# Indexer products and sums per pair of heads in a two-layer decoder trunk

## Chip, cores and metric

One core of one Trainium2 chip. The metric is device time in microseconds (us), the median of three executions of one launch.

## The reference

A decoder trunk of two layers on x of 512 tokens by 1024 channels, all in float32: a gated linear recurrence (HGRN2) and a convolutional FFN, then sparse attention (DSA) and a second FFN, and a final norm. The change lies in the sparse attention, whose indexer picks for each query the 128 keys (512 // 4) that it may attend to:

```python
proj = x @ w_in                       # q 1024 | k 128 | v 128 | q_idx 512 | k_idx 64 | w_idx 8
dots = jnp.einsum('bthd,bsd->bths', qib, k_idx)                      # 8 index heads of 64
scores = jnp.einsum('bths,bth->bts', jax.nn.relu(dots), wb)          # sum over the heads
scores = jnp.where(admissible[None], scores, NEG_BIG)                # causal
_, sel = lax.top_k(scores, top_k)
```

The 16 attention heads then take a softmax over the selected keys, with a bias by relative position.

## The kernel before, in words

Every float32 matrix product is made of three `fp32r` matmuls (high times high, high times low, low times high), so a projection block of 128 output channels is 24 matmuls of 128x512 on TensorE (`proj_T`, lines 169 to 171, tile `pj`). Its weight block comes by DMA (`wunit`, line 150) and is split into `whi` and `wlo`. From the projection of k on, ScalarE makes `whi` (L159) and a negative copy (L158), and a DMA on GpSimd's queue adds the weights once more onto that (L160).

TensorE runs its instructions in the order in which the program writes them (`manual_schedule`). That order comes from generators: `weave` runs a main generator, and after each step lets the generators in `side` advance by as much assumed time as the step had; a generator that needs something waits until a name stands in `done`. The order on the other engines is set by the scheduler of the language, which also places all waits.

The sparse layer goes like this:

- `head_in` projects k_idx and w_idx (72 channels), then the four pairs of index heads (b = 0 to 3, 128 channels each). After each pair, `stack` (L675 to L678) writes the pair's two heads as stacked high and low halves into `qh` and `ql`: two copies on ScalarE (L675, L676), then two subtractions on VectorE (L677 ends `qh`, L678 ends `ql`). `kw_evac` (L696, L704 to L706) does the same for the keys, and `kw_weights` turns the weights of the heads (L713, L715).
- `dots`, added to `side` when `head_in` is over, goes through the query blocks t = 1, 2, 3 of 128 queries each; block 0 needs no selection. For a block it goes through the four pairs: four matmuls into two PSUM banks `pi` (L749), a relu on ScalarE (L759), and a multiply-add into the block's sum `sc[t]` on VectorE (L755 for the first head, L760 for the others). Then GpSimd masks the block (L762).
- `top` finds the 128 largest by 16 rounds of MAX (8 largest, L774) and MATCH_REPLACE (L776) on VectorE, first for block 1, then for blocks 2 and 3; at the end a mask `sel1`, `sel2`, `sel3` is written (L779).
- `rest_in` projects k, v and the eight query blocks q0 to q7; each block's PSUM is read by a scaling row on VectorE (`scaled`, L696).
- `attend`, woven into the rest of these projections, takes attention in units of two query blocks and two heads: `scores` (L860 adds the mask by a matmul, L863 multiplies), a biased minimum on VectorE (L870), exponents on ScalarE, and later transposes (L912, L915), copies (L916) and the product with v (L923, L926).

The lines around which the change turns are these:

```python
def head_in():
    pk = yield from proj_T(w_in, O_KI, 72)
    for b in range(4):
        o = yield from proj_T(w_in, O_QI + b * P, hook=({7: lambda: kw_evac(pk)}, {2: kw_weights}, None, None)[b])
        lo_engine[0] = nc.gpsimd
        stack(4 + b, o, nc.vector)
```

Of the kernel before, what the change touches and what calls it, by code (L numbers as in the profile page):

```python
# [8 lines left out]
F32 = mybir.dt.float32  # L9
# [3 lines left out]
AF = mybir.ActivationFunctionType  # L13
ALU = mybir.AluOpType
# [3 lines left out]
P = 128  # L18
D = 1024
T = 512  # L20
# [3 lines left out]
NEG = -1e30  # L24
# [24 lines left out]
def trunk(ctx: ExitStack, tc: tile.TileContext, xT, vecs, convs, hgrn_w_in, hgrn_w_out, dsa_w_in, dsa_w_out,  # L49
          rel_bias, ffn_w_up, ffn_w_down, c_masks, c_onehot, out, dbg=None, stop=99):  # L50
    nc = tc.nc
# [9 lines left out]
    def bank(name):  # L61
        return ps.tile([P, 512], F32, name=name, tag="bank")
# [110 lines left out]
    def proj_T(w, c0, n=P, hook=None):  # L173

        wh, wl = wunit(w[:, c0:c0 + n], KB, n)
        o = bank("pj")
        for k in range(KB):
            mm3(o[:n], wh[:, k, :], wl[:, k, :], xh[:, k, :], xl[:, k, :], k == 0, k == KB - 1)
            yield 0.65
            if hook and k in hook:  # L180
                hook[k]()
        return o


    side, done = [], set()

    def add_side(gen, rate=1.0):
        side.append([gen, rate, 0.0])
# [8 lines left out]
    def weave(gen):  # L197
        for c in gen:
            for e in list(side):
                e[2] += c * e[1]  # L200
                while e in side and e[2] > 0:
                    step(e)
# [458 lines left out]
    with ExitStack() as sx:  # L661
        ds_ = sx.enter_context(tc.tile_pool(name="ds", bufs=1))
        bias = ds_.tile([P, AH, T], F32, name="bias")
        qh = ds_.tile([P, KB, T], F32R, name="qh")
        ql = ds_.tile([P, KB, T], F32R, name="ql")
# [5 lines left out]
        def stack(b, src, lo):  # L671

            a, c = qh[:, b, :], ql[:, b, :]
            top_, bot = rows2
            nc.scalar.activation(a[top_], src[top_], AF.Copy)  # L675
            nc.scalar.activation(c[bot], src[bot], AF.Copy)  # L676
            lo.tensor_tensor(a[bot], src[top_], a[top_].bitcast(F32), op=ALU.subtract)  # L677
            lo.tensor_tensor(c[top_], src[bot], c[bot].bitcast(F32), op=ALU.subtract)  # L678
# [4 lines left out]
        wN = ds_.tile([P, TT, 8], F32, name="wN")  # L683
        scs = ds_.tile([P, 9 * P], F32, name="scs")
        sc = [None, scs[:, 7 * P:], scs[:, 4 * P:7 * P], scs[:, :4 * P]]
        m8 = ds_.tile([P, TT, 8], F32, name="m8")

        with ExitStack() as sy:
            iy = sx.enter_context(tc.tile_pool(name="iy", bufs=1))
            ix = sy.enter_context(tc.tile_pool(name="ix", bufs=1))  # L690
            ki_h = ix.tile([P, T], F32R, name="ki_h")
            ki_l = ix.tile([P, T], F32R, name="ki_l")
# [8 lines left out]
            def kw_evac(o):  # L701
                tmp = scaled(o, 72)
                for r in (slice(0, 64), slice(64, 128)):
                    nc.scalar.activation(ki_h[r], tmp[:64], AF.Copy)  # L704
                nc.vector.tensor_tensor(ki_l[:64], tmp[:64], ki_h[:64].bitcast(F32), op=ALU.subtract)
                nc.vector.tensor_tensor(ki_l[64:], tmp[:64], ki_h[:64].bitcast(F32), op=ALU.subtract)  # L706
                kw.append(tmp)

            def kw_weights():
                tmp = kw.pop()  # L710
                pw = bank("pw")
                for t in range(TT):
                    nc.tensor.transpose(pw[:, t * 72:(t + 1) * 72], tmp[:72, t * P:(t + 1) * P], ident[:72, :72])  # L713
                for t in range(TT):
                    nc.vector.tensor_scalar(wN[:, t, :], pw[:, t * 72 + 64:(t + 1) * 72], 8 ** -0.5 * 64 ** -0.5,  # L715
                                            rstd_c[:, t:t + 1], op0=ALU.mult, op1=ALU.mult)

            def setup():

                yield 7.0  # L720
                nc.vector.tensor_copy(identb, ident)
                nc.gpsimd.memset(vf, 0.0)
                for h in range(0, AH, 4):
                    nc.scalar.activation(bias[:, h:h + 4, :256], far[:, h:h + 4, None].to_broadcast([P, 4, 256]),
                                         AF.Copy, scale=-1.0)

                    back = ix.tile([P, 4, 256], F32, name="back", bufs=2)
                    nc.sync.dma_start(back, bass.AP(tensor=Z.tensor, offset=Z.offset + h * BAND,
                                                    ap=[[1, P], [BAND, 4], [1, 256]]))
                    nc.scalar.activation(bias[:, h:h + 4, 256:], back[:, :, ::-1], AF.Copy)  # L730
                    yield 3.0
# [4 lines that stand above are left out]
                    o = yield from proj_T(w_in, O_QI + b * P,  # L736
                                          hook=({7: lambda: kw_evac(pk)}, {2: kw_weights}, None, None)[b])
                    lo_engine[0] = nc.gpsimd
                    stack(4 + b, o, nc.vector)

            def dots():
                for t in range(1, TT):
                    w = (t + 1) * P
                    ts_ = slice(t * P, (t + 1) * P)
                    for b in range(4):
                        o = [bank("pi") for _ in range(2)]
                        for k_ in (ki_h, ki_l):
                            for e in range(2):
                                nc.tensor.matmul(o[e][:, :w], (qh, ql)[e][:, 4 + b, ts_], k_[:, :w],  # L749
                                                 start=k_ is ki_h, stop=k_ is ki_l)  # L750
                        yield 0.22 * (t + 1)
                        for e in range(2):
                            i = 2 * b + e
                            if i == 0:
                                nc.vector.tensor_scalar(sc[t], o[e][:, :w], 0.0, wN[:, t, 0:1],  # L755
                                                        op0=ALU.max, op1=ALU.mult)
                            else:
                                r_ = ix.tile([P, T], F32, name="relu", bufs=2)
                                nc.scalar.activation(r_[:, :w], o[e][:, :w], AF.Relu)  # L759
                                nc.vector.scalar_tensor_tensor(sc[t], r_[:, :w], wN[:, t, i:i + 1], sc[t],  # L760
                                                               op0=ALU.mult, op1=ALU.add)
                    nc.gpsimd.affine_select(sc[t][:, w - P:], sc[t][:, w - P:], pattern=[[-1, P]], base=0,  # L762
                                            channel_multiplier=1, compare_op=ALU.is_ge, fill=NEG)
                    done.add(f"sc{t}")
                    if t == 1:
                        add_side(top((1,)), 0.4)

            def top(ts):

                while any(f"sc{t}" not in done for t in ts):  # L770
                    yield 0.5
                for r in range(16):
                    for t in ts:
                        nc.vector.max(m8[:, t, :], sc[t])  # L774
                    for t in ts:
                        nc.vector.match_replace(sc[t], m8[:, t, :], sc[t], -3e38)  # L776
                    yield sum(2 * (0.065 + (t + 1) * P / 960) for t in ts)
                for t in ts:
                    nc.vector.tensor_scalar(sel[t], sc[t], -2e38, -NEG, op0=ALU.is_gt, op1=ALU.mult)  # L779
                    done.add(f"sel{t}")  # L780
                if 3 not in ts:
                    add_side(top((2, 3)), 0.55)
# [16 lines left out]
            def rest_in():  # L799
                lo_engine[0] = None  # L800
                pk = yield from proj_T(w_in, O_K)
                pv = yield from proj_T(w_in, O_V, hook={3: lambda: k_out(pk)})
                for b in range(KB):
                    lo_engine[0] = nc.vector if b >= 6 else None
                    o = yield from proj_T(w_in, b * P, hook={3: lambda: kw.append(scaled(pv)), 7: v_out}
                                          if b == 0 else None)
                    tmp = scaled(o, P, -0.125)
                    stack(b, tmp, nc.gpsimd)
                    done.add(f"q{b}")
                done.add("q8")  # L810

            add_side(norm_chain())
            add_side(setup())
            weave(head_in())
            add_side(dots(), 1.0)
            rest = rest_in()
            for c in rest:
                weave([c])
# [220 lines left out]
```

## Time and profile before

| | |
|---|---|
| Median of three executions | 1273.68 us (1273.42 to 1275.24) |
| The profiled execution | 1276.48 us, of which the span from first to last instruction is 1274.7 us |
| Mean granted TensorE clock | 0.997 of full speed |
| Busy, share of the span | TensorE 98%, VectorE 63%, ScalarE 47%, GpSimd 11% |
| Sparse layer | its projections begin at 668 us, its last products with v start at 852 us |

In a timeline row the first number is the start in us from the span's start, the second the length, then engine, line, operation, written and read tiles, sizes; a bracket at the end is idle time of that engine just before, and what ended it. A matmul's end is modelled, so a row of 0.39 us may be followed by the next start 0.23 us after its own. Waits are inferred from semaphore events.

### The profile page before, as it was taken

How to read it: one execution, taken by the hardware profiler on the slowest of the kernel's cores; microseconds unless marked ns; L12 is line 12 of the kernel's file. 1: busy time of each engine (PE TensorE's matmuls, PEld its weight loads, DVE VectorE, ACT ScalarE, POOL GpSimd, SP SyncE). 2: the span in 40 equal slices, each digit the busy share in tenths (PEclk: the TensorE clock that was granted, in tenths of full speed). 3: DMA queues.
4: the chain of work that ended last, by engine and by line, in shares of the span. 5: the costliest groups of instructions: out<-in, count | busy, mean ns of one | idle time of the engine just before them, and what ended most of it. 6: DMA issues, size and time to landing. Idle time of an engine off the chain costs nothing.

```text
span 1274.7 us, 15695 instructions
## 1 busy us (share of the span) xinstructions
PE 1251.4 (98%) x6054; PEld 1046.2 (82%) x6054; DVE 803.0 (63%) x1305; ACT 599.6 (47%) x989; POOL 138.8 (11%) x120
## 2 busy tenths in 40 slices
PE   8999999999999999999999998999999999999997
PEld 7788888887888888888887777988888888888887
DVE  7755777756777777742444999635677777762331
ACT  5546565444544444421337757853444444441430
POOL 3022223110000000000003453300000000000000
PEclk9999999999999999999999999999999999999999
DMA  6339777323333333322237850003233333333222
GB/s 199 117 73 158 133 129 126 76 66 99 91 93 98 99 99 99 98 91 93 87 103 173 134 109 25 27 1 99 83 100 99 99 99 94 92 95 99 91 75 66
DMA packets 199178, 124.05 MB, mean 97 GB/s; under 512 B 5264, under 2 KB 188480, under 8 KB 199104
## 3 DMA queue, kind: packets, MB, share of 16 engines
q1 hardware_dynamic: 170320, 108.31, 28.7%
q0 software_dynamic: 28080, 14.16, 9.3%
q8 instruction: 47, 0.77, 0.3%
q10 hardware_dynamic: 704, 0.58, 0.2%
q14 instruction: 27, 0.22, 0.1%
HBM read 120.92 MB, written 2.12 MB: 97 GB/s over the span
## 4 chain that ended last, share of the span: by engine, by line
PE 88%; DVE 7%; ACT 2%; issue 1%; DMA 0%; POOL 0%; DVEq 0%; SPq 0%; POOLq 0%; ACTq 0%
PE pj L169 17%; PE pj L171 17%; PE pj L170 17%; PE px L169 9%; PE px L171 9%; PE px L170 9%; PE pav L923 2%; DVE scs L776 2%; PE pl L556 1%; PE po L602 1%; DVE m L774 1%; DVE scs L760 1%; PE pl L863 1%; PE pt L912 1%; PE pn L170 1%
## 5 line engine op out<-in xcount | busy, mean ns | idle before, releaser
L169 PE MATMUL pj<-x,whi 128*128 128x512 f32 (+1 forms) x1016 | 403.0, 397 | 0.0
L171 PE MATMUL pj<-x,wlo 128*128 128x512 f32 (+1 forms) x1016 | 396.9, 391 | 1.1 <-DMA wlo<-in_dsa_w_in_dram 1.1
L170 PE MATMUL pj<-x,whi 128*128 128x512 f32 (+1 forms) x1016 | 396.3, 390 | 0.0
L144 DVE TENSOR_TENSOR wlo<-wr,whi 128x1024 fp32r<-128x1024 f32 (+2 forms) x165 | 202.0, 1224 | 155.1 <-ACT whi L143 153.1
L143 ACT ACTIVATE whi<-wr 128x1024 fp32r<-128x1024 f32 (+1 forms) x167 | 173.6, 1039 | 257.1 <-PE px L170 155.2
L171 PEld LDWEIGHTS pj<-x,wlo 128*128 128x128 f32 (+1 forms) x1016 | 190.6, 188 | 42.4 <-DMA wlo<-in_dsa_w_in_dram 1.5
L169 PEld LDWEIGHTS pj<-x,whi 128*128 128x128 f32 (+1 forms) x1016 | 191.0, 188 | 39.2 <-issue 1.6
L170 PEld LDWEIGHTS pj<-x,whi 128*128 128x128 f32 (+1 forms) x1016 | 191.1, 188 | 38.8 <-issue 1.0
L169 PE MATMUL px<-ah,whi 128*128 128x512 f32 (+1 forms) x332 | 128.5, 387 | 0.0
L171 PE MATMUL px<-ah,wlo 128*128 128x512 f32 (+1 forms) x332 | 127.5, 384 | 0.0
L170 PE MATMUL px<-al,whi 128*128 128x512 f32 (+1 forms) x332 | 126.2, 380 | 0.0
L348 DVE TENSOR_TENSOR ub<-pj,rstd_r 128x512 f32<-128x512 f32 x88 | 60.6, 688 | 82.3 <-PE pj L171 77.3
L143 ACT ACTIVATE ah<-c 128x512 fp32r<-128x512 f32 x44 | 27.8, 631 | 115.9 <-DVE c L360 115.9
L171 PEld LDWEIGHTS px<-ah,wlo 128*128 128x128 f32 x332 | 62.3, 188 | 13.5
L170 PEld LDWEIGHTS px<-al,whi 128*128 128x128 f32 x332 | 62.3, 188 | 12.8
L351 ACT ACTIVATE c<-ub,convc 128x512 f32<-128x512 f32 x88 | 71.2, 809 | 2.4 <-DVE ub L348 1.6
L169 PEld LDWEIGHTS px<-ah,whi 128*128 128x128 f32 x332 | 62.4, 188 | 11.4
L353 DVE SCALAR_TENSOR_TENSOR c<-ub,convc,c 128x512 f32<-128x512 f32 x88 | 66.2, 752 | 3.0
L358 ACT ACTIVATE c<-c 128x512 f32<-128x512 f32 x44 | 27.8, 632 | 80.8 <-DVE c L353 80.7
L352 DVE SCALAR_TENSOR_TENSOR c<-ub,convc,c 128x512 f32<-128x512 f32 x88 | 65.6, 746 | 0.0
L522 DVE TENSOR_TENSOR qk<-qk,ftree 128x512 f32<-128x512 f32 x56 | 39.6, 709 | 17.6 <-PE pl L560 7.1
L144 DVE TENSOR_TENSOR al<-c,ah 128x512 fp32r<-128x512 f32 x44 | 30.4, 692 | 29.3 <-ACT ah L143 29.3
(226 smaller groups left out, 1743.9 us busy)
## 6 DMA issues: line engine op xcount, KB each, us to landing
wr<-in_ffn_w_up_dram SPq DMA_DIRECT2D x88, 512.0 KB, 3.8
wr<-in_ffn_w_down_dram SPq DMA_DIRECT2D x41, 512.0 KB, 3.7
wr<-in_hgrn_w_in_dram SPq DMA_DIRECT2D x30, 512.0 KB, 4.1
wlo<-in_hgrn_w_in_dram POOLq DMA_DIRECT2D x19, 512.0 KB, 7.5
wr<-in_dsa_w_in_dram SPq DMA_DIRECT2D x14, 512.0 KB, 3.7
wr<-in_hgrn_w_out_dram SPq DMA_DIRECT2D x8, 512.0 KB, 3.6
wlo<-in_dsa_w_in_dram POOLq DMA_DIRECT2D x8, 512.0 KB, 7.8
wr<-in_dsa_w_out_dram SPq DMA_DIRECT2D x8, 512.0 KB, 3.8
```

The lines of the kernel that those rows point to most:

```text
L143: nc.scalar.activation(dst_h, src, AF.Copy)
L144: lo.tensor_tensor(dst_l, src, dst_h.bitcast(F32), op=ALU.subtract)
L169: nc.tensor.matmul(o, ah, bh, start=start, stop=False)
L170: nc.tensor.matmul(o, ah, bl, start=False, stop=False)
L171: nc.tensor.matmul(o, al, bh, start=False, stop=stop)
L348: nc.vector.tensor_tensor(u[:, 2:], o, rows(), op=ALU.mult)
L351: nc.scalar.activation(c, u[:, 2:], AF.Identity, scale=cc[2], bias=cc[3])
L352: nc.vector.scalar_tensor_tensor(c, u[:, 1:T + 1], cc[1], c, op0=ALU.mult, op1=ALU.add)
L353: nc.vector.scalar_tensor_tensor(c, u[:, 0:T], cc[0], c, op0=ALU.mult, op1=ALU.add)
L358: nc.scalar.activation(g, g, AF.Silu)
L522: nc.vector.tensor_tensor(turned(m), turned(m), factors(ft, m), op=ALU.mult)
L776: nc.vector.match_replace(sc[t], m8[:, t, :], sc[t], -3e38)
```

## The change

`dots` becomes a generator of one pair: it goes through the three query blocks for that pair, and is added to `side` as soon as the pair is projected and its `stack` is written, in place of once after `head_in`. It waits until the heads' weights are there (`done.add("wN")`). The mask of a block, and the start of `top`, follow the last pair. The matmuls, relus, sums and masks are the same in number and size.

```diff
@@ kw_weights
                                             rstd_c[:, t:t + 1], op0=ALU.mult, op1=ALU.mult)
+                done.add("wN")
@@ head_in
                     stack(4 + b, o, nc.vector)
-
-            def dots():
+                    add_side(dots(b))
+
+            def dots(b):
+
+                while "wN" not in done:
+                    yield 0.3
                 for t in range(1, TT):
                     w = (t + 1) * P
                     ts_ = slice(t * P, (t + 1) * P)
-                    for b in range(4):
-                        o = [bank("pi") for _ in range(2)]
-                        for k_ in (ki_h, ki_l):
-                            for e in range(2):
-                                nc.tensor.matmul(o[e][:, :w], (qh, ql)[e][:, 4 + b, ts_], k_[:, :w],
-                                                 start=k_ is ki_h, stop=k_ is ki_l)
-                        yield 0.22 * (t + 1)
...
+                    o = [bank("pi") for _ in range(2)]
+                    for k_ in (ki_h, ki_l):
                         for e in range(2):
+                            nc.tensor.matmul(o[e][:, :w], (qh, ql)[e][:, 4 + b, ts_], k_[:, :w],
+                                             start=k_ is ki_h, stop=k_ is ki_l)
+                    yield 0.22 * (t + 1)
...
+                    if b == 3:
+                        nc.gpsimd.affine_select(sc[t][:, w - P:], sc[t][:, w - P:], pattern=[[-1, P]], base=0,
+                                                channel_multiplier=1, compare_op=ALU.is_ge, fill=NEG)
+                        done.add(f"sc{t}")
+                        if t == 1:
+                            add_side(top((1,)), 0.4)
@@
             weave(head_in())
-            add_side(dots(), 1.0)
             rest = rest_in()
```

Lines of the changed kernel: the product is L753 there, the first head's sum L759, the relu L763, the other sums L764, MAX L779, MATCH_REPLACE L781, the masks L784, the biased minimum L874.

**First place: TensorE in the projection of pair 1**, after the transposes of the heads' weights (`pw`, L713), which follow that projection's ninth matmul. Before:

```order
L171 MATMUL pj<-x,wlo 128x512
L713 MATMUL pw<-ident,tmp 128x72 x4
L169 MATMUL pj<-x,whi 128x512
L170 MATMUL pj<-x,whi 128x512
L171 MATMUL pj<-x,wlo 128x512
L169 MATMUL pj<-x,whi 128x512
```

And now:

```order
L171 MATMUL pj<-x,wlo 128x512
L713 MATMUL pw<-ident,tmp 128x72 x4
L169 MATMUL pj<-x,whi 128x512
L170 MATMUL pj<-x,whi 128x512
L171 MATMUL pj<-x,wlo 128x512
L753 MATMUL pi<-ki_h,qh 128x256
L753 MATMUL pi<-ki_h,ql 128x256
L753 MATMUL pi<-ki_l,qh 128x256
L753 MATMUL pi<-ki_l,ql 128x256
```

The first products of pair 0 stand three projection matmuls after `pw`. For pairs 1, 2 and 3 the first products stand three matmuls after the end of that pair's own projection. Before, the first of all products stood three matmuls after the end of pair 3's.

**Second place: VectorE before the mask `sel1`** (`sel_5019`). Before, from the scaling row of q2 on:

```order
L696 SCALAR_TENSOR_TENSOR tmp<-pj,rstd_r 128x512
L774 MAX m_5025<-scs 128x8
L776 MATCH_REPLACE scs<-m_5025,scs 128x512
L776 MATCH_REPLACE scs<-m_5025,scs 128x256
L774 MAX m_5025<-scs 128x8
L779 TENSOR_SCALAR sel_5019<-scs 128x256
```

And now:

```order
L779 MAX m_5025<-scs 128x8
L781 MATCH_REPLACE scs<-m_5025,scs 128x512
L781 MATCH_REPLACE scs<-m_5025,scs 128x256
L696 SCALAR_TENSOR_TENSOR tmp<-pj,rstd_r 128x512
L784 TENSOR_SCALAR sel_5019<-scs 128x256
L779 MAX m_5025<-scs 128x8 x2
```

`sel1` now follows the scaling row of q2 at once. On TensorE its first reader stands 6 matmuls after the end of q2's projection, where it stood 12 after it.

**Third place: VectorE before the masks `sel2` and `sel3`** (`sel_5020`, `sel_5021`). Now the scaling row of q7, the first line here, is followed by:

```order
L696 SCALAR_TENSOR_TENSOR tmp<-pj,rstd_r 128x512
L781 MATCH_REPLACE scs<-m_5025,scs 128x384
L781 MATCH_REPLACE scs<-m_5025,scs 128x512
L874 ISA L_5943,mn<-pl,bias 128x128
L874 ISA mn 128x1
L874 ISA L_5945,mn<-pl,bias 128x128
L874 ISA mn 128x1
L874 ISA L_5947,mn<-pl,bias 128x256
L874 ISA mn 128x1
L874 ISA L_5949,mn<-pl,bias 128x256
L874 ISA mn 128x1
L784 TENSOR_SCALAR sel_5020<-scs 128x384
```

Before, the biased minima of four units, in place of one, stood between q7's scaling row and the masks, with rounds of `top` among them; the masks came here:

```order
L776 MATCH_REPLACE scs<-m_5025,scs 128x384
L776 MATCH_REPLACE scs<-m_5025,scs 128x512
L890 RECIPROCAL sm<-sm 128x4
L144 TENSOR_TENSOR ql<-on,qh 128x256
L891 COPY rs<-sm 128x256
L779 TENSOR_SCALAR sel_5020<-scs 128x384
L779 TENSOR_SCALAR sel_5021<-scs 128x512
```

The masks of blocks 2 and 3 have moved forward by three units of attention in VectorE's order.

## Rows read from the trace of the kernel before

**Rows 1.** The page: busy us, share of the span and instructions of each engine.

```profile
PE 1251.4 (98%) x6054; PEld 1046.2 (82%) x6054; DVE 803.0 (63%) x1305; ACT 599.6 (47%) x989; POOL 138.8 (11%) x120
```

**Rows 2.** Timeline of TensorE (PE): four of its waits between 700 and 800 us.

```profile
724.32 0.66 PE L796 MATMUL pt<-ident,tmp 128*128 128x128 f32 x4 [0.60 <-DVE tmp L696]
...
732.00 0.50 PE L171 MATMUL pj<-x,wlo 128*128 128x512 f32 x1 [1.10 <-DMA wlo<-in_dsa_w_in_dram]
...
742.62 0.38 PE L860 MATMUL pl<-sel,identb 128*128 128x256 bf16 x2 [2.14 <-DVE sel L779]
...
788.71 0.50 PE L860 MATMUL pl<-sel,identb 128*128 128x384 bf16 x2 [1.77 <-DVE sel L779]
```

**Rows 3.** Timeline of TensorE: the places of the products, new and old.

```profile
684.75 0.40 PE L169 MATMUL pj<-x,whi 128*128 128x512 f32 x1
...
688.18 0.39 PE L169 MATMUL pj<-x,whi 128*128 128x512 f32 x1
...
693.62 0.39 PE L169 MATMUL pj<-x,whi 128*128 128x512 f32 x1
...
699.06 0.28 PE L749 MATMUL pi<-ki_h,qh 128*128 128x256 f32 x1
...
701.89 0.28 PE L749 MATMUL pi<-ki_h,qh 128*128 128x256 f32 x1
702.26 0.36 PE L749 MATMUL pi<-ki_h,ql 128*128 128x256 f32 x1
...
714.49 0.39 PE L749 MATMUL pi<-ki_l,ql 128*128 128x512 f32 x1
```

**Rows 4.** Timeline of ScalarE (ACT) at the end of pair 1's projection.

```profile
687.53 1.06 ACT L159 ACTIVATE whi<-wr 128x1024 fp32r<-128x1024 f32 x1 [1.93 <-issue]
...
689.22 0.59 ACT L676 ACTIVATE ql<-pj 64x512 fp32r<-64x512 f32 x1
```

**Rows 5.** Timeline of VectorE (DVE): the keys' low half, then the last subtraction of pairs 0 to 3.

```profile
683.77 2.47 DVE L705 TENSOR_TENSOR ki_l<-tmp,ki_h 64x512 fp32r<-64x512 f32 x1 [0.77 <-ACT ki_h L704]
...
688.06 0.69 DVE L678 TENSOR_TENSOR ql<-pj,ql 64x512 fp32r<-64x512 f32 x1
...
690.56 0.69 DVE L678 TENSOR_TENSOR ql<-pj,ql 64x512 fp32r<-64x512 f32 x1
...
695.98 0.69 DVE L678 TENSOR_TENSOR ql<-pj,ql 64x512 fp32r<-64x512 f32 x1
...
701.42 0.69 DVE L678 TENSOR_TENSOR ql<-pj,ql 64x512 fp32r<-64x512 f32 x1
```

**Rows 6.** Chain that ended last, 720 to 765 us: start, us on the chain, what.

```profile
723.67 0.59 DVE tmp L696
...
730.77 0.33 DVE m L774
...
737.22 0.40 DVE scs L776
...
741.90 0.67 DVE sel L779
...
762.15 1.05 DVE m L774 x2
763.20 1.19 DVE scs L776 x2
```

**Rows 7.** Busy time by stretch of 1 us; PEclk is the granted TensorE clock.

```profile
743.00:744.00 1.00, 1.00 (x7) 0.90 (x7) 1.00 (x6) 0.08 (x1) 0.77 (x1) 0.87 1.21 144
744.00:745.00 1.00, 1.00 (x3) 0.80 (x3) 1.00 (x8) 0.94 (x5) 0.00 (x0) 0.50 1.46 181
...
747.00:748.00 1.00, 1.00 (x5) 0.79 (x5) 0.08 (x1) 0.33 (x1) 0.00 (x0) 0.92 0.00 0
```

**Rows 8.** Timeline of TensorE in that stretch: two projection matmuls in a row.

```profile
744.22 0.63 PE L169 MATMUL pj<-x,whi 128*128 128x512 f32 x1
744.64 0.63 PE L170 MATMUL pj<-x,whi 128*128 128x512 f32 x1
```

More of the change, by code (lines that the diff above doesn't have):

```diff
@@ L744, in dots @@
                     ts_ = slice(t * P, (t + 1) * P)
-                    for b in range(4):
-                        o = [bank("pi") for _ in range(2)]
-                        for k_ in (ki_h, ki_l):
-                            for e in range(2):
-                                nc.tensor.matmul(o[e][:, :w], (qh, ql)[e][:, 4 + b, ts_], k_[:, :w],
-                                                 start=k_ is ki_h, stop=k_ is ki_l)
-                        yield 0.22 * (t + 1)
-                        for e in range(2):
[L753 to L766, printed above, removed]
+                    o = [bank("pi") for _ in range(2)]
+                    for k_ in (ki_h, ki_l):
+                        for e in range(2):
+                            nc.tensor.matmul(o[e][:, :w], (qh, ql)[e][:, 4 + b, ts_], k_[:, :w],
+                                             start=k_ is ki_h, stop=k_ is ki_l)
@@ new lines, in dots @@
+                    yield 0.22 * (t + 1)
+                    for e in range(2):
+                        i = 2 * b + e
+                        if i == 0:
+                            nc.vector.tensor_scalar(sc[t], o[e][:, :w], 0.0, wN[:, t, 0:1],
+                                                    op0=ALU.max, op1=ALU.mult)
+                        else:
+                            r_ = ix.tile([P, T], F32, name="relu", bufs=2)
+                            nc.scalar.activation(r_[:, :w], o[e][:, :w], AF.Relu)
+                            nc.vector.scalar_tensor_tensor(sc[t], r_[:, :w], wN[:, t, i:i + 1], sc[t],
+                                                           op0=ALU.mult, op1=ALU.add)
```

## The prediction

> **What bounds the kernel now.** The page comes first: TensorE is busy 98% of the span [rows 1], so time is lost or won only where TensorE waits, or where its clock is down. Its timeline shows where it waits in the sparse layer: 0.60 us for the scaled v, 1.10 us for a weight DMA, 2.14 us for `sel1`, 1.77 us for `sel2` [rows 2]. Such idle time is counted from a matmul's modelled end. Projection matmuls start 0.227 us apart (24 of them from 693.62 to 699.06, [rows 3]) and their rows are 0.39 us long, so each wait costs 0.16 us more than its idle time: 0.76, 1.26, 2.30 and 1.93 us. The stretches of 1 us show the last thing: after the wait for `sel1` the granted clock falls to 0.50 from 743.7 to 747.2 us, some 3.4 us [rows 7]. That is 1.2 GHz in place of 2.4: matmuls then start 0.42 us apart [rows 8], so 8 are done in place of 15, and the fall costs 7 x 0.227 = 1.6 us.
>
> VectorE's share is 63%, but the chain between 720 and 765 us runs through it, round after round of MAX and MATCH_REPLACE [rows 6]. The change gives VectorE its sums sooner; the question is what TensorE pays for it.
>
> **The change, part by part.** *Moved products.* All 48 product matmuls stay, at the same size: 0 us by themselves. But TensorE keeps the written order, and now the products of a pair stand three projection matmuls behind that pair's projection. Whether `qh` and `ql` are written by then can be read from the trace of before, since ScalarE and VectorE write them in the same order.
>
> - Pair 0: TensorE would issue the first product at 684.75 [rows 3]. `ql` is finished at 688.06 + 0.69 = 688.75 [rows 5], and a product follows such an end after 0.15 us: 701.42 + 0.69 = 702.11 in [rows 5], 702.26 in [rows 3]. The first product (0.12 us) fits in before. Lost: 688.90 - 0.12 - 684.75 = 4.03 us.
> - Pair 1: the place is 688.18 [rows 3], `ql` ends at 691.25 [rows 5]. Lost: 691.40 - 0.12 - 688.18 = 3.10 us. ScalarE shows why: it first makes the next weights (687.53, 1.06 us), which wait for the same end of projection, and its second copy of the pair ends at 689.81 [rows 4]; two subtractions of VectorE follow.
> - Pair 2: 693.62 [rows 3] against 696.67 [rows 5], by the same sum 3.08 us. Pair 3: 699.06 against 702.11, again 3.08 us.
>
> Sum: **13.3 us** of new waits. In the old order other matmuls stood there, and covered all but 0.25 us of pair 3's (701.89 to 702.26, less 0.12, [rows 3]); that is taken off.
>
> *Relus and sums moved.* The relus of pair b stand on ScalarE behind that pair's copies and ahead of the next ones; six relus at most, done within the next projection of 5.4 us. They cost 0 while a projection covers them, and without that cover would add to the next pair's wait. On GpSimd's queue all three masks now stand ahead of the weight DMA of q1; they end with the last sums, before the projection of k frees that DMA's buffer, so they cost 0; SP's queue is unchanged.
>
> *What VectorE makes of it.* After the last product (call its slot e), VectorE needs some 5.1 us until the scaling row of k: the last two sums, four MAX and three MATCH_REPLACE. By the order, between that row and `sel1` stand 13 rounds of block 1 (0.33 + 0.40 us each, [rows 6]), 5 pairs of MAX (1.05) and 6 of MATCH_REPLACE (1.19) of blocks 2 and 3, and five scaling rows (0.6): 9.5 + 5.3 + 7.1 + 3.0 = 24.9 us. With `sel1` itself (0.67) and 0.15 us it is there at e + 30.8. The same prices give 17.5 us from the end of the row at 723.67 to 741.90, which took 17.6 [rows 6]. TensorE reaches the mask after 120 projection matmuls (27.3), four transposes and four products (0.7), at e + 28.0. So it **waits 2.8 us** for `sel1` again. Bounds: 0, if rounds interleave better than counted, and twice that.
>
> *Later waits.* The waits for v, for the DMA and the old one for `sel1` fall away: 0.76 + 1.26 + 2.30 us. (ScalarE's relus no longer hold back the copies ahead of that DMA; if it should still be late, it only takes from the wait for `sel1`.) `sel2` and `sel3` now stand one unit behind q7's scaling row, in place of four; TensorE needs them some 15 us after that projection, so 1.93 us go. Next after it come shorter waits for ScalarE's copies of transposes, left as they are.
>
> Without the clock: 13.3 - 0.25 - 0.76 - 1.26 - 2.30 + 2.8 - 1.93 = **+9.6 us**.
>
> *The clock.* A wait of 2.14 us brought one fall, 1.77 us brought none [rows 2, 7]. Pair 0's wait is some 3.2 us in one piece, since the two subtractions end 0.7 us apart; those of pairs 1 to 3 are 2.3 us and then 0.4. The first lies well above the row, the others barely. I count two falls ahead of pair 3's wait, 2 x 1.6 = +3.2 us; bounds 0 and 3 x 1.6 = 4.8. One behind pair 3's wait would mostly be taken out of the wait for `sel1`, and the one behind `sel1` was there before: together 0. The Trainium skill ("TensorE: Matmul & The Clock Gate", section "Why this matters for your kernels") warns of idle gaps in mid-kernel, but of ones longer than all here except pair 0's; by it one fall would be counted (+1.6, in sum +11.2), while the row after 2.14 us speaks for more.
>
> Sum: 9.6 + 3.2 = **+12.8 us** on the profiled execution of 1276.48 us, or 1289.3. The median of the runs, 1273.68, lies 2.8 us lower; from there it is **1286.5 us**.
>
> **The rivals.**
>
> 1. *The clock falls once or not at all.* For it: only one wait is clearly longer than the one of 2.14 us. Against: all four are longer. 1273.7 + 9.6 = 1283.3, or 1284.9 with one fall. The rule named above makes it 1284.9, by the same rows.
> 2. *Early waits are paid back.* If VectorE is 2.8 us quicker than counted, because it works on while TensorE stands still, the wait for `sel1` goes as well: +6.8 us and up to two falls, 1280.5 to 1283.7. It decides whether the 24.9 us fit into the 22 us from k's to q2's projection. Against: the same prices hold for 17.6 us of before.
> 3. *Faster.* The operands of each pair are ready in time, and VectorE's idle time before 702 us goes into sums. Then all of [rows 2] and the fall vanish: 6.25 + 1.6, or 1265.8 us. It needs `ql` written within 0.7 us of the end of a projection; the rows have 3.8 (687.5 to 691.25, [rows 4, 5]). ScalarE's and VectorE's orders at this place are as before, so little speaks for it.
> 4. *No change.* The order shows the products moved, so only gains that happen to equal the waits are left: within 2.5 us.
>
> **How the numbers follow.** Chances: the forecast, with two falls or more, 0.56; rival 1, 0.24; rival 2, 0.13; faster 0.03; no change 0.03; 0.01 for more than four falls. 0.2% of this time is 2.5 us. All of the first three are slower by over that: 0.94. The range goes from rival 2's lower part, 1280, to 1291.5, the forecast with three falls (1288.1) and 3.4 us for a wait for `sel1` longer than counted. What it leaves out: faster, no change, and the tails, below 0.2 in sum.
>
> **What would show it.** In the changed profile TensorE should show idle time before L753 with VectorE's L678 as its end, twice per pair, nearly 12 us in all, and stretches at clock 0.50 behind the first of them. L801 and the DMA of q2 should show no wait; the wait before L864 for `sel1` should be near 2.6 us, the one for `sel2` gone. VectorE's idle time between 686 and 702 us should hold sums. Wrong would be: waits before L753 under 1 us (then the copies run in another order than counted), or no wait before L864 at all (rival 2).

## The result, and the profile after

The changed kernel takes **1288.76 us** (median of four executions, 1287.27 to 1292.47), the kernel before 1273.68 beside it. The ratio is 1.0120, with a 95% interval from 1.0095 to 1.0145: some 15 us slower between the medians, where +12.8 was forecast. The profiled execution took 1290.08 us, its span is 1288.2 us (before: 1274.7), so between the two traces 13.5 us have to be explained.

The page's line of engines. TensorE is as full as before [rows 1], VectorE and ScalarE do the same work in a longer span:

```profile
PE 1257.6 (98%) x6054; PEld 1050.0 (82%) x6054; DVE 803.8 (62%) x1305; ACT 599.4 (47%) x989; POOL 136.0 (11%) x120
```

TensorE's waits in the changed kernel (engine, waiting operation and line, what it waits for: us in total, times, longest):

```profile
PE pi L753 <- DVE qh L677: 9.4, 4, 3.1
PE pl L864 <- DVE sel L784: 2.1, 1, 2.1
PE pav L927 <- ACT px L920: 1.9, 2, 1.0
PE pi L753 <- DVE ql L678: 1.5, 4, 0.4
PE pt L919 <- DVE rs L895: 1.0, 1, 1.0
```

The products now stand at the head of the list. Each pair waits twice, first for `qh`, then for `ql`; together that is 10.9 us of idle time. The waits for v, for the weight DMA of q2 and for `sel2` [rows 2] are gone. The one for `sel1` is there again.

TensorE's timeline in the changed kernel: the last projection matmul ahead of pair 0's and pair 1's products, with both waits of these pairs, then the first wait of pairs 2 and 3, the last product of all, and the wait for `sel1`:

```profile
682.43 0.40 PE L171 MATMUL pj<-x,wlo 128*128 128x512 f32 x1
685.91 0.38 PE L753 MATMUL pi<-ki_h,qh 128*128 128x256 f32 x1 [3.09 <-DVE qh L677]
686.73 0.36 PE L753 MATMUL pi<-ki_h,ql 128*128 128x256 f32 x1 [0.43 <-DVE ql L678]
...
693.57 0.39 PE L171 MATMUL pj<-x,wlo 128*128 128x512 f32 x1
696.04 0.38 PE L753 MATMUL pi<-ki_h,qh 128*128 128x256 f32 x1 [2.08 <-DVE qh L677]
696.86 0.36 PE L753 MATMUL pi<-ki_h,ql 128*128 128x256 f32 x1 [0.43 <-DVE ql L678]
...
708.20 0.58 PE L753 MATMUL pi<-ki_h,qh 128*128 128x256 f32 x1 [2.10 <-DVE qh L677]
...
721.54 0.38 PE L753 MATMUL pi<-ki_h,qh 128*128 128x256 f32 x1 [2.10 <-DVE qh L677]
...
726.17 0.39 PE L753 MATMUL pi<-ki_l,ql 128*128 128x512 f32 x1
...
756.88 0.38 PE L864 MATMUL pl<-sel,identb 128*128 128x256 bf16 x2 [2.14 <-DVE sel L784]
```

From such rows the price of a pair follows as in the prediction. Pair 0's first product could have started at 682.43 + 0.23 = 682.66, the second one starts at 686.73, and the first takes 0.12 of that: 3.95 us lost. Pairs 1 to 3 lose 2.94, 2.95 and 2.95 by the same sum. In all 12.8 us.

Where the time of pair 1 goes stands in the timeline of ScalarE and VectorE of the changed kernel. It is the chain of [rows 4, 5], in the same order: first the next weights, then two copies, then two subtractions:

```profile
693.13 1.06 ACT L159 ACTIVATE whi<-wr 128x1024 fp32r<-128x1024 f32 x1 [1.32 <-PE pj L170]
694.10 0.57 ACT L675 ACTIVATE qh<-pj 64x512 fp32r<-64x512 f32 x1
694.68 0.59 ACT L676 ACTIVATE ql<-pj 64x512 fp32r<-64x512 f32 x1
...
695.30 0.68 DVE L677 TENSOR_TENSOR qh<-pj,qh 64x512 fp32r<-64x512 f32 x1 [2.71 <-ACT ql L676]
696.02 0.69 DVE L678 TENSOR_TENSOR ql<-pj,ql 64x512 fp32r<-64x512 f32 x1
```

The busy time by stretch of 1 us (us, then busy time of PE, PEld, DVE, ACT and POOL with instructions, PEclk, DMA share, GB/s), behind the waits of pairs 0, 1 and 2, and in the last line behind the wait for `sel1`:

```profile
687.00:688.00 1.00, 1.00 (x8) 1.00 (x7) 0.64 (x2) 0.39 (x1) 0.00 (x0) 0.84 0.00 0
688.00:689.00 1.00, 1.00 (x4) 0.81 (x4) 0.90 (x3) 0.49 (x1) 0.00 (x0) 0.50 0.00 0
...
699.00:700.00 1.00, 1.00 (x4) 0.81 (x3) 0.90 (x2) 0.44 (x1) 0.00 (x0) 0.50 0.94 146
...
709.00:710.00 1.00, 0.98 (x4) 1.00 (x5) 0.00 (x0) 0.18 (x1) 0.89 (x1) 0.50 0.26 50
...
714.00:715.00 1.00, 1.00 (x4) 0.74 (x3) 0.49 (x1) 0.96 (x2) 0.00 (x0) 0.51 1.40 176
...
757.00:758.00 1.00, 1.00 (x8) 0.95 (x7) 1.00 (x3) 0.96 (x3) 0.80 (x1) 1.00 0.80 293
```

Busy time in longer stretches, same columns: two of the changed kernel, then the second one in the kernel before:

```profile
686.00:702.00 16.00, 13.05 (x46) 10.37 (x47) 8.67 (x16) 7.39 (x13) 1.61 (x1) 0.79 0.34 63
702.00:726.00 24.00, 19.14 (x69) 15.38 (x68) 9.54 (x17) 10.58 (x18) 3.39 (x3) 0.79 0.48 80
```

```profile
702.00:726.00 24.00, 23.30 (x110) 19.37 (x109) 23.39 (x52) 18.80 (x33) 8.54 (x8) 1.00 0.65 107
```

VectorE has its first sums early, between 686 and 702 us, but from 702 to 726 it is busy for 9.54 of 24 us, where the kernel before shows 23.39: its next sums need the products of pairs 2 and 3, and these stand behind two more projections and their waits.

From the rows of 1 us: the granted clock is 0.50 for 3.4 us behind pair 0, 3.4 behind pair 1, 6.8 behind pair 2 and 3.4 behind pair 3: 17 us, where the kernel before had 3.4 us, behind its wait for `sel1` [rows 7]. Behind the wait for `sel1` of the changed kernel, just as long at 2.14 us, the clock stays full.

**The books.** New waits 12.8, less pair 3's old 0.25; the old waits of [rows 2] gone, -6.25; `sel1` again, 2.14 + 0.16 = +2.3; three waits for copies in attention (0.96 and 0.95 us for `px`, 1.03 for `rs`, in place of 0.79, 0.49 and 0.56, all for `px`), +1.1. That is +9.7 us. Five stretches at half clock in place of one add 4 x 1.6 = 6.4. From this 2.1 us are taken, by which this execution was early ahead of the change: the same matmul (L240) starts at 671.29 us, at 673.43 in the trace of before. The sum is +14.0; the spans differ by 13.5. In the eleven traces of the experiments, whose code is the same up to there, that start lies anywhere from 671.7 to 673.4, so the 2.1 us are put down to the execution and not to the change.

### The profile page after: what moved, and what is told of

Its sections match the earlier page's. It is cut to its first block, busy times and chain, and to the rows that moved or that the text cites. A ratio compares the mean times of both kernels' runs of the same rounds, so it can differ in the third digit from the quotient of the medians.

```text
span 1288.2 us, 15693 instructions
## 1 busy us (share of the span) xinstructions
PE 1257.6 (98%) x6054; PEld 1050.0 (82%) x6054; DVE 803.8 (62%) x1305; ACT 599.4 (47%) x989; POOL 136.0 (11%) x120
## 4 chain that ended last, share of the span: by engine, by line
PE 90%; DVE 5%; issue 2%; ACT 1%; DMA 1%; POOL 0%; DVEq 0%; POOLq 0%; SPq 0%; ACTq 0%
PE pj L169 16%; PE pj L170 16%; PE pj L171 16%; PE px L169 9%; PE px L171 9%; PE px L170 8%; PE pav L927 2%; PE pl L556 2%; PE pl L867 1%; DVE scs L781 1%; PE po L602 1%; PE pt L916 1%; DVE m L779 1%; PE pn L170 1%; PE pi L753 1%
## 5 line engine op out<-in xcount | busy, mean ns | idle before, releaser
L171 PEld LDWEIGHTS px<-ah,wlo 128*128 128x128 f32 x332 | 62.3, 188 | 13.5
L170 PEld LDWEIGHTS px<-al,whi 128*128 128x128 f32 x332 | 62.4, 188 | 12.7
```

What stands on the lines that cost most here:

```text
L170: nc.tensor.matmul(o, ah, bl, start=False, stop=False)
L171: nc.tensor.matmul(o, al, bh, start=False, stop=stop)
```

## The experiments

All kernels are the changed one with the edit that is shown (e5 has e4's edit as well, e9 has e1's). Lines in their traces lie a few higher or lower. Ratios are to the kernel before, run beside them on the same chip. e5 to e8 ran on another chip than the other experiments, so between these two groups the ratios are compared rather than the times.

### Where the products stand: e1_later, e2_some

The theory: what costs is the place of a pair's products in TensorE's written order, three matmuls behind a projection whose halves need 3.8 us more. Behind the wait for the heads' weights a pause of assumed time is put in:

```diff
                 while "wN" not in done:
                     yield 0.3
+                yield 4.0 if b == 0 else 3.3
```

> The changed kernel, but each pair's products are put off until its ql is written: 18 projection matmuls after the end of the pair's projection in place of 3 (pair 0: 15 later than in the change). Theory (the products stand in TensorE's order ahead of their operands): the waits before L753, 10.9 us of idle time in the changed kernel, go below 1.5 us in sum, and no stretch at clock 0.50 stands between 680 and 725 us. The wait for sel1 stays near 2.8 us, the one for sel2 stays gone: 1273.7 - 0.25 - 0.76 - 1.26 - 2.30 + 2.8 - 1.93 = 1270 us. Rival (the change is slow because VectorE's sums are regrouped and block 1's rounds start later): the sums keep their grouping here, so the time stays near 1283 to 1289 us.

Measured: 1270.36 us (1270.3 to 1270.88), ratio 0.9960 [0.9946, 0.9975]. No product waits, no stretch at half clock; it beats both kernels. TensorE's waits in its timeline between 700 and 760 us:

```profile
729.50 0.50 PE L171 MATMUL pj<-x,wlo 128*128 128x512 f32 x1 [0.76 <-DMA wlo<-in_dsa_w_in_dram]
741.51 0.38 PE L865 MATMUL pl<-sel,identb 128*128 128x256 bf16 x2 [1.47 <-DVE sel L785]
```

With a pause that is too short for the halves (`yield 1.4`):

> The changed kernel, with each pair's products put off by 6 projection matmuls (9 after the end of the pair's projection, in place of 3), that is 1.36 us. Theory: each of the four waits shrinks by 1.36 us and no more, so the idle time before L753 falls from 10.9 to about 5.5 us; the longest piece is then below 2 us, so the clock falls at most once, behind pair 0. Time: 1288.8 - 5.5 - 7 = 1276 us, or 1278 with one fall. If the clock falls as often as in the change, 1283 us.

Measured: 1278.80 us (1277.61 to 1280.03), ratio 1.0029 [1.0019, 1.0039]. The waits before the products shrink to 1.38 and 0.43 us for pair 0, 0.43 for pair 1, 0.74 and 0.43 for pairs 2 and 3, and none is followed by a fall. That is 2.8 us more than the 1276 expected without a fall: the 7 us that the expectation takes off for the clock were read from the one trace, and e3 and e11 below show that they are too much for the median. The three placements, 1288.8, 1278.8 and 1270.4 us, come in the order of the waits of the products: 12.8 us; 6.1 us by the same sum (2.24, 0.63, 1.60 and 1.60 for the four pairs); none. The steps of the medians, 10.0 and 8.4 us, are larger than those of the waits. In the first the falls of the clock go as well; what is left of the second was not followed up.

### Which pair: e6_pair0, e7_pairs123

Only pair 0's products are placed later (`if b == 0: yield 2.6`), or only the others (`if b > 0: yield 3.3`).

> Only the products of pair 0 stand four steps (12 projection matmuls, 2.7 us) later than in the changed kernel (1288.8 us); those of pairs 1 to 3 stand where the change puts them. Theory: each wait of 2 us or more is paid where it is and brings its own fall of the clock. Then pair 0's wait goes from 4.0 to 1.3 us, too short for a fall, so 2.7 + 1.6 us go: 1284.5 us; the stretches at half clock behind pairs 1 to 3 stay. Rival 1: pair 0's long wait starts all the falls, and without it there is none: some 2.7 + 8 us go, 1278 us. Rival 2: what is won comes back at the wait for sel1: 1287 to 1289 us.

Measured: 1280.56 us (1279.02 to 1281.65), ratio 1.0053 [1.0040, 1.0067]: better than the theory's 1284.5. Pair 0 waits 0.43 us, and so does pair 1, since pair 0's products now stand behind the projection of pair 1 and cover its wait. That step was missing in the expectation. What is left are the waits of pairs 2 and 3, as long as in the changed kernel. Only the first of the two was followed by a stretch at half clock. That there is one at all speaks against rival 1 (pair 0's wait starts all the falls). The two waits, and the windows behind them:

```profile
701.56 0.38 PE L755 MATMUL pi<-ki_h,qh 128*128 128x256 f32 x1 [2.10 <-DVE qh L677]
...
713.74 0.38 PE L755 MATMUL pi<-ki_h,qh 128*128 128x256 f32 x1 [2.10 <-DVE qh L677]
```

```profile
703.00:704.00 1.00, 1.00 (x5) 1.00 (x5) 0.52 (x2) 0.61 (x2) 1.00 (x1) 0.50 0.93 257
...
716.00:717.00 1.00, 1.00 (x6) 0.83 (x5) 0.90 (x2) 0.84 (x2) 0.48 (x2) 1.00 1.13 334
```

> The other part: pair 0's products stand where the change puts them, those of pairs 1 to 3 some 3.4 us later. Theory: the waits of pairs 1 to 3 go (3 x 2.85 = 8.5 us with their start-up) and with them the four stretches at half clock behind them (4 x 1.6 = 6.4 us); pair 0's 4 us and its one stretch stay. 1288.8 - 14.9 = 1274 us by that, 1276 us counted up from e1 (1270.4 + 4.0 + 1.6). Rival: the falls follow pair 0's wait, and stay when the others go: 1280 us.

Measured: 1277.46 us (1277.01 to 1280.16), ratio 1.0034 [1.0021, 1.0048]. Pair 0 waits 2.90 and 0.43 us, one stretch of 3.4 us at half clock follows, and none comes later: the falls belong to the waits just ahead of them, and the rival (1280) falls. The time is 1.5 us above the upper sum of the expectation.

### The clock without the waits: e3_fill

In place of each pair's wait TensorE gets matmuls of constants into a bank that nobody reads, 17 ahead of pair 0's products and 13 ahead of the others (56 x 0.227 = 12.7 us):

```diff
+                fill = bank("fill")
+                for _ in range(17 if b == 0 else 13):
+                    nc.tensor.matmul(fill, ones_r, ones_r[:, None, :].to_broadcast([P, 4, P]), start=True, stop=True)
```

> The changed kernel, with 17 (pair 0) or 13 (pairs 1 to 3) matmuls of constants, which nobody reads, ahead of each pair's first product: 3.9 and 3.0 us, about as long as TensorE waits there. It separates the price of the clock from the price of the waits. Theory: the time at the four places stays lost, but the stretches at clock 0.50 (17 us of them in the changed profile) go, except that the last one was partly paid back by a shorter wait for sel1: 1288.8 - 7 = 1282 us. Rival (the low clock runs beside the waits and costs nothing of its own): 1288 to 1289 us. If the clock had been the whole loss, 1274 us.

Measured: 1286.03 us (1285.41 to 1286.69), ratio 1.0082 [1.0067, 1.0097]: between theory and rival. No product waits, and no fall comes behind any of them. One does come behind `sel1`, whose wait is as long as in the changed kernel, where none came. Wait and stretch of e3, from its timeline and its windows:

```profile
751.74 0.38 PE L867 MATMUL pl<-sel,identb 128*128 128x256 bf16 x2 [2.14 <-DVE sel L787]
```

```profile
753.00:754.00 1.00, 1.00 (x5) 0.77 (x4) 1.00 (x8) 0.99 (x2) 0.93 (x2) 0.58 1.07 119
754.00:755.00 1.00, 1.00 (x4) 0.81 (x3) 1.00 (x4) 1.00 (x5) 0.68 (x1) 0.50 1.23 150
```

So the idle time brings the falls. But between the medians of the changed kernel and e3 lie 2.7 us; with the 1.6 of e3's own fall that makes all falls of the changed kernel worth about 4 us, and not the 5 x 1.6 = 8 us of the one trace. So the changed kernel was run again.

### The same kernel again: e11_again

> The changed kernel once more, unaltered. So far waits of 2.08 to 2.19 us of TensorE were followed by a fall of the clock in six places of these traces and by none in six others; waits of 2.9 us and more always were, waits of 1.9 us and less never. Theory: at about 2.1 us it depends on the execution, so in this one the waits stand where they stood and are as long, but the stretches at half clock behind the products of pairs 1 to 3 need not come at the same places; the one behind pair 0's 3.1 us does. Rival: the place in the program decides, and the stretches repeat exactly (one behind pairs 0, 1 and 3, a double one behind pair 2, none behind sel1). Time in both cases 1286 to 1291 us.

Measured: 1287.23 us (1286.95 to 1290.92), ratio 1.0109 [1.0091, 1.0127]. The waits are the same to 0.1 us, 3.19, 2.10, 2.09 and 2.10 us and 2.14 for `sel1`; the falls are not. Two stretches come, behind pairs 0 and 1 (3.4 us each); behind pairs 2 and 3 the clock stays full, where the first trace had 10.2 us at half. The rival falls. In the windows of e11 behind pair 0, and at pair 2's products:

```profile
689.00:690.00 1.00, 1.00 (x4) 0.90 (x4) 0.83 (x2) 0.42 (x1) 0.00 (x0) 0.50 0.00 0
...
709.00:710.00 1.00, 0.49 (x2) 0.32 (x3) 0.72 (x2) 0.39 (x1) 0.01 (x1) 1.00 0.00 0
710.00:711.00 1.00, 1.00 (x7) 1.00 (x8) 0.18 (x1) 0.59 (x2) 1.00 (x1) 1.00 0.38 59
```

This execution took 1286.95 us. Its books: waits 12.9 by the same sum, less 0.25 and 6.25, `sel1` 2.3, copies 1.1: +9.8. One stretch more than before, +1.6, and 1.3 us early at the start: +10.1, where the spans differ by 1285.1 - 1274.7 = 10.4.

### Why VectorE's early start brings nothing at sel1: e4_regroup, e5_regroup_split

Two things are in the change: products by pair, and earlier. The first alone: the four pairs' generators run one behind the other, after `head_in`, where the old `dots` ran.

```diff
-                    add_side(dots(b))
...
+            def all_dots():
+                for b in range(4):
+                    yield from dots(b)
+
+            add_side(all_dots())
```

> The kernel before, with the loops turned alone: after all four pairs are projected, the products go pair by pair through the three query blocks, in place of block by block. No product is taken earlier than before. Theory (regrouping itself is harmless, the early place costs): no wait before L753 above 0.5 us, no new fall of the clock, the wait for sel1 2 to 3 us, sel2 without a wait: 1270 to 1273 us. Rival (regrouping costs, since block 1 is complete only with the last pair and its 16 rounds start some 8 us later): 1277 to 1281 us, with a wait for sel1 of 6 us or more.

Measured: 1279.23 us (1277.91 to 1281.31), ratio 1.0033 [1.0023, 1.0043]. The size is the rival's, the place is neither's: TensorE waits 4.84 us for a weight DMA, 6.8 us at half clock begin during that wait, and then it waits 2.19 us for `sel1`. e4's timeline of TensorE, then of GpSimd's queue, where the DMA is issued:

```profile
728.01 0.77 PE L171 MATMUL pj<-x,wlo 128*128 128x512 f32 x1 [4.84 <-DMA wlo<-in_dsa_w_in_dram]
```

```profile
719.30 1.57 POOL L160 DMA_DIRECT2D wlo<-in_dsa_w_in_dram  x1 [2.22 <-ACT wlo L158]
```

It waits for ScalarE's negative copy of the weights (L158), which came at 717.88 us, behind relus and the copies of the keys; in the kernel before it came at 711.84. To see whether that is all, the weights of q1 are split on GpSimd, without copy and DMA:

```diff
-                    lo_engine[0] = nc.vector if b >= 6 else None
+                    lo_engine[0] = nc.vector if b >= 6 else nc.gpsimd if b == 1 else None
```

> The kernel of e4 (grouping per pair, all after the head projections), with the weights of q1 split on GpSimd in place of ScalarE's negative copy and the adding DMA. e4: 1279.2 us, with a wait of 4.84 us for that DMA (ScalarE's copy for it came at 717.9 us, behind the relus and the copies of the keys, in place of 711.8 in the kernel before) and 6.8 us at half clock around it. Theory: grouping per pair is harmless by itself; what e4 loses against the kernel before comes from that late transfer. Then 4.84 + 0.16 of waiting and some 2.3 us of half clock behind it go, less about 1 us for q2's transfer, which is next: 1272 to 1273 us, with the wait for sel1 at 2 to 3 us. Rival: TensorE only reaches the mask of block 1 earlier and waits there instead, since VectorE sets that time: wait for sel1 6 us or more, 1277 to 1279 us.

Measured: 1279.01 us (1278.05 to 1281.48), ratio 1.0045 [1.0031, 1.0059]. The wait for the DMA is gone, and nearly all of it stands before the mask of block 1: 6.24 us there, where e4 had 4.84 and 2.19. The rival holds. e5's last product, and that wait:

```profile
712.70 0.40 PE L752 MATMUL pi<-ki_l,ql 128*128 128x512 f32 x1
...
748.65 0.58 PE L869 MATMUL pl<-sel,identb 128*128 128x256 bf16 x2 [6.24 <-DVE sel L783]
```

VectorE's timeline of e5 shows the reason:

```profile
709.77 5.43 DVE L763 SCALAR_TENSOR_TENSOR scs<-relu,wN,scs 128x384 f32<-128x384 f32 x4
714.73 0.48 DVE L763 SCALAR_TENSOR_TENSOR scs<-relu,wN,scs 128x256 f32<-128x256 f32 x1
715.53 1.01 DVE L763 SCALAR_TENSOR_TENSOR scs<-relu,wN,scs 128x256 f32<-128x256 f32 x2 [0.33 <-ACT relu L762]
716.73 0.43 DVE L778 MAX8 m<-scs 128x8 f32<-128x256 f32 x1 [0.19 <-POOL scs L766]
```

By blocks, block 1's sum is whole first, and GpSimd masks it at 706.70 us, while the other blocks' products still run. By pairs, every block's sum is whole only with the last pair: block 1's last sums end at 716.5, and its first MAX starts at 716.73, at 707.33 in the kernel before. TensorE gets `sel1` at 748.65, 6.0 us later than at 742.62 [rows 2]. That is what the grouping costs. In the changed kernel the first three pairs' products are earlier as well, and that pays most of it back. From the start of the last product to the start of the mask that reads `sel1` it is 742.62 - 714.49 = 28.1 us before [rows 2, 3], 748.65 - 712.70 = 36.0 in e5, and 756.88 - 726.17 = 30.7 in the changed kernel. The wait for `sel1` comes out at 2.14 us before and after.

### The wait for sel1 itself: e8_enough, e9_mask_later, e10_later_again

e8 is e1 with a pause one step shorter (`yield 3.4 if b == 0 else 2.7`).

> As e1, with the products 2.7 (pair 0: 3.4) in place of 3.3 (4.0) units of assumed time later: one step of three matmuls earlier than in e1. Theory: this is just enough for the stacked halves (in e2, two or three steps earlier still, 1.2 us were missing for pairs 2 and 3 and 1.8 for pair 0; 1.4 and 2.0 us are added), so no product waits; VectorE gets the last sums 0.7 us sooner, and the wait for sel1 falls from 1.5 to about 0.8 us: 1269.5 to 1270.5 us. Rival: some halves are still 0.4 us late, 1272 us; or the other waits (copies of transposes) grow by what sel1 gives, and it stays at 1270.4.

Measured: 1273.29 us (1272.11 to 1274.85), ratio 0.9998 [0.9989, 1.0007]. No product waits, but the gain at `sel1` did not come: that wait is 2.13 us, and those for copies grew (1.81, 0.90, 0.67 and 0.57 us; in e1 1.24 and 1.87). The theory was wrong there; of the rival, the second half names the right waits, but the time lies above both its numbers. Why one step earlier costs that much against e1 (ratio 0.9998, not 0.9960) stays open. So e1's 1270.4 was in question, and it was run again, beside a kernel in which TensorE reads `sel1` later, as the search is assumed to be slower:

```diff
-                            add_side(top((1,)), 0.4)
+                            add_side(top((1,)), 0.36)
```

> The kernel of e1 once more, beside e9 on the same chip: 1270.4 us was measured; e8, one step earlier, took 1273.3 us beside another set of runs. Theory: no wait for products, ratio to the kernel before 0.996 again. Rival: e1 and e8 differ by the chip they ran on only, and the ratio is 0.998 to 1.000.

> As e1 (products 3.3 to 4.0 units of assumed time later), and the search for the largest 128 of block 1 is assumed to go slower (rate 0.36 in place of 0.4), so that TensorE reads sel1 five steps (some 3.4 us) later. Theory: the wait for sel1 is a question of where its reader stands in TensorE's order, and costs what it shows; e1's wait of 1.47 us (1.6 with start-up) goes, nothing else changes: e1 less 1.6 us, about 1269 us. Rival: attention as a whole starts later and is squeezed at the end, so that the waits for copies of transposes and for sel2 take it back: as e1 or up to 2 us slower.

Measured: e10 1270.69 us (1270.31 to 1274.13), ratio 0.9977 [0.9967, 0.9986]; e9 1269.47 us (1269.19 to 1272.97), ratio 0.9967 [0.9955, 0.9979]. For e10 the ratio came out between the theory's 0.996, which lies outside its interval, and the rival's 0.998, which lies inside: e1's place gains some 3 us, and 5 us as first measured is too much. Of e10's eleven executions six took 1270.3 to 1270.7 us and five 1272.2 to 1274.1. The profiled one is of the second sort, 1.9 us above e1's. About 1.1 us of that lie ahead of the sparse layer (L240 starts at 673.31 us, at 672.25 in e1). The rest is at `sel1`, as its timeline and windows show:

```profile
742.38 0.58 PE L865 MATMUL pl<-sel,identb 128*128 128x256 bf16 x2 [2.38 <-DVE sel L785]
```

```profile
743.00:744.00 1.00, 1.00 (x5) 0.95 (x5) 0.75 (x4) 0.00 (x0) 0.00 (x0) 0.50 0.43 51
```

In e1 TensorE lost 0.76 us to a DMA and 1.47 us to `sel1`, here 2.38 us at once. With 0.16 us for each wait both are 2.5 us, but the one wait of 2.38 us came with a fall, and the two short ones did not. In e9 no wait for `sel1` is left, and no fall; its median is 1.2 us below e10's, where 1.6 was expected. The intervals of e9 and e10 overlap, so that gain is not shown. Both beat the kernel before.

## Why the prediction was right

The forecast, slower by 12.8 us, was right in sign, place and nearly in size; the median lies 2.3 us above the 1286.5, inside the range, and e11's 0.7 us above. The closeness is in part luck, as two of the steps show. (For the chance of being slower, 0.94, the first three add up to 0.93; the rest is the 0.01 for more than four falls.) By its own steps:

- **Moved products, 13.3 us: right.** 12.8 us in the first trace, 12.9 in the second. Pair 0 was put at 4.03 and measured 3.95 and 4.05; pairs 1 to 3 were put at 3.1 and measured 2.95, since ScalarE's and VectorE's order at that place was as read from [rows 4, 5]. Of a pair's two waits the first ends at L677, not at L678 as foreseen. e1 and e2 show that the place was the cause.
- **Relus, masks and queues, 0: right.** No wait in TensorE's list of the changed kernel ends at one of them.
- **Old waits, -6.25: right.** The waits for v, for the DMA of q2 and for `sel2` are gone.
- **`sel1` again, 2.8 us: right, a little high.** 2.3 us. The mask's reader was put 30.8 us after the last product and starts 30.7 us after it, so rival 2 (no wait at `sel1`) is out. e5 gives the reason that the prediction did not: by pairs, block 1's sum is no longer whole first.
- **Shorter waits for copies "left as they are": wrong by 1.1 us.** Three of them grew to about 1 us each. It cancels the 0.5 each by which the pairs and `sel1` were too high, so that the part without the clock, forecast at +9.6, measured +9.7 and +9.8. That it agrees so closely is luck.
- **The clock, +3.2: right in kind, and no single number.** Two falls ahead of pair 3 were counted, and the one behind `sel1` kept. The first trace had four such stretches and pair 3's, and none behind `sel1`, net +6.4, outside the bounds of 0 to 4.8; the second had the two, and none behind `sel1`, net +1.6. That the forecast lies between the two is luck as well. The step that failed is the rule behind it, that a wait as long as the 2.14 us of before brings a fall: it may. The Trainium skill ("TensorE: Matmul & The Clock Gate", section "Why this matters for your kernels") warns of idle gaps in mid-kernel that are longer than all of these waits except pair 0's; by it only that one would have brought a fall. These traces disagree: behind 2.08 and 2.10 us at pair 1 the clock fell in both.
- **The faster rival, 1265.8:** its condition, operands ready in time, was made true by e1 and e9 by moving the place. They took 1270.4 and 1269.5, not 1265.8, since other waits of 0.8 to 1.9 us each (for a DMA, for copies of transposes, in e1 for `sel1`) came in the place of the old ones.

## What to carry to other kernels

Before work is moved forward on the engine that bounds, read from the trace when its operands are written, and put it that much later in the written order: here a pause of five or six steps of three matmuls turned a loss of 15 us into a gain of 3 to 5 us (ratios 0.9977 and 0.9960), with the same regrouping. Where several results are summed in turn, look at which one is needed first: summing all of them together makes the first as late as the last.

## What had not been expected of the hardware

- **Equal waits, unequal clock.** In the sparse layer of the traces shown or told of here, TensorE idled 17 times for 2.08 to 2.38 us (once before, four times each in the changed kernel and in e11, three times in e6, once each in e2, e3, e4, e8 and e10); eight of these waits came with a stretch at half clock, nine did not, and for pairs 2 and 3 the same wait of the same program was in one execution and was not in the other. All five waits of 2.9 us or more came with one (2.90, 3.09, 3.19, 4.84 and 6.24 us; in the last two the clock fell while TensorE still waited), none of 1.9 us or less did. What decides between 2.08 and 2.38 us stays open.
- **Two short waits and one of about their sum.** 0.76 and 1.47 us (e1's trace) came with no fall, 2.38 us (e10's) with one, in the same program. It is one case of each: since equal waits of this length differ, it does not show that splitting a wait saves the fall.
